# A hybrid decoder layer on one core: column order, chain engines, inverse blocks and PSUM tiles of the RWKV stage rewritten

## The chip, the cores and the metric

The kernel runs on one core of one Trainium2 chip. The metric is the device time of one launch in microseconds (us). A kernel's time is the median of its runs; beside it there is one execution taken with the hardware profiler, whose own time can differ a little from the median.

## The reference

One layer of a decoder for a prompt of 1024 rows and for 8 single decode rows, all in float32. The rows are normalised and go through one projection `w_in` (1024 to 3480 columns). Its columns feed three groups of heads:

- NSA: 8 query heads with compressed, selected and sliding-window attention, mixed by gates.
- RWKV-7: 4 heads with a state of 64 x 64 each.
- memory: 4 heads that attend to 256 memory rows.

Each group's output is multiplied by the SiLU of its gate columns; one output projection follows, and the residual is added. The part that matters here is the RWKV group, which the reference computes row by row:

```python
u = u_cur + (prev - u_cur) * mu            # token shift
r, k, v, wl, al = split(u)
decay = exp(-exp(w)); a = sigmoid(a0 + al @ a2)
def step(s, inp):
    r_t, k_t, v_t, w_t, kk_t, b_t = inp
    sa = einsum('bhvk,bhk->bhv', s, -kk_t)
    s = s * w_t + sa[..., None] * b_t + v_t[..., None] * k_t
    return s, einsum('bhvk,bhk->bhv', s, r_t)
```

Queries and keys of the other groups get a root-mean-square norm per head of 64, a gain, and rotary positions (rope).

## The kernel before

Phase 1 does the projection and the RWKV group; phase 2 the attention of the prompt, with most of the decode rows as side work; phase 3 the rest of the decode rows.

**Projection.** The 1024 prompt rows are taken in two halves H of 512. A column block of 128 is loaded by `wblock` (L227 on): one DMA of 512 KB, then the float32 weights are split into a high part on ScalarE (whi, L236) and a low part (wlo, L238), six eighths of it on GpSimd and two on VectorE. `project` (L241 on) runs eight steps; in each the three products hi*hi, hi*lo and lo*hi of one eighth of the 1024 inputs are added into PSUM. The p_pr tiles come from a pool of three one-bank buffers; a column needs two of them for H = 0 (512 prompt and 8 decode rows) and one for H = 1. After the eighth step the column is evicted: `do_u` for the seven RWKV columns (ScalarE copies, VectorE adds the shifted row, and the copy to ulast, L283, is last), `to_tok` for the others (ScalarE copies; later, in the next column's third step, four TensorE transposes to token order and then `kv_rows` or `norm_rope` and a DMA to DRAM), or `do_z` for gate columns.

**Norm and rope.** `norm_rope` (L307 on) squares on ScalarE, sums and takes the reciprocal root on VectorE, multiplies by it on VectorE (L323), by the gain on GpSimd (L324), and makes four products with sine and cosine on GpSimd (L334 to L337), which VectorE combines (L338, L339).

**RWKV in chunks.** The prompt is taken in four chunks Q of 256 rows. `rwkv_prep` (L572 on) makes the scaled rows and the masked product matrix AM; some of its elementwise steps run on GpSimd. `rwkv_state` (L682 on) inverts eight triangular matrices of 64 x 64. They are held as blocks of 32; five rounds double the inverted size (p_iy, then p_it with the new inverse T and its transpose Tt in one tile), and two more products join the blocks of 32 (tile iO, L745). The inverse is applied in p_x (L769 to L773), and four steps of 64 rows carry the state Z (p_z, L807 to L811). U, the RWKV input, holds two chunks: its first half is projected before chunk 0, its second half while chunk 1's state runs.

**The order of the work.** From chunk 0 until the fill is used up, TensorE's instructions are chained in the order in which the program emits them (class `InOrder`, whose helper line is L83 in the profile). The other engines are ordered by the framework's planner. `drive` (L489 on) runs a chunk's generator: each `yield n` says how long the chain behind it needs, and 1.3 n units of other columns (the fill, 0.7 units per step) are emitted there. Of the 21 column blocks outside RWKV, 16 are fill; what is left after chunk 3 is emitted in one go. `rwkv_out` (normalisation of the chunk's output) is emitted inside the next chunk's prep.

**The end of phase 1.** The last five columns run with background work of 41 steps (keys, compression, and memory keys, `ahead`, L478): after each group of eight column steps, BG = 4 background steps are emitted. Then phase 2 starts with the scores of its first tile and the compressed scores p_sc (L1151).

Of the kernel before, what the change touches and what calls it, by code (L numbers as in the profile page):

```python
# [31 lines left out]
BG = 4  # L32
# [70 lines left out]
class Step:  # L103
# [203 lines left out]
    def norm_rope(self, x, gain, nt, nh, rope, parts=128, psum=True):  # L307
# [16 lines left out]
        nc.gpsimd.tensor_tensor(y, y, bc(self.gains[:parts, gain:gain + 1, :], [parts, n, 64]), op=OP.mult)  # L324
# [4 lines left out]
        y4 = y.rearrange("p (t h) (s e) -> p t h s e", h=nh, s=2)  # L329
        o4 = o.rearrange("p (t h) (s e) -> p t h s e", h=nh, s=2)  # L330
        s4 = sq.rearrange("p (t h) (s e) -> p t h s e", h=nh, s=2)
        sh = [parts, nt, nh, 32]
        cos, sin = bc(cs[..., 0:32], sh), bc(cs[..., 32:64], sh)
        nc.gpsimd.tensor_tensor(s4[:, :, :, 0], y4[:, :, :, 1], sin, op=OP.mult)  # L334
        nc.gpsimd.tensor_tensor(s4[:, :, :, 1], y4[:, :, :, 0], sin, op=OP.mult)
        nc.gpsimd.tensor_tensor(o4[:, :, :, 0], y4[:, :, :, 0], cos, op=OP.mult)
        nc.gpsimd.tensor_tensor(o4[:, :, :, 1], y4[:, :, :, 1], cos, op=OP.mult)  # L337
        nc.vector.tensor_tensor(o4[:, :, :, 0], o4[:, :, :, 0], s4[:, :, :, 0], op=OP.subtract)  # L338
        nc.vector.tensor_tensor(o4[:, :, :, 1], o4[:, :, :, 1], s4[:, :, :, 1], op=OP.add)  # L339
# [52 lines left out]
    def phase1(self):  # L392
# [8 lines left out]
        with ExitStack() as ctx:  # L401
# [104 lines left out]
    def columns(self, tiles):  # L506
        rest = None
        for c0, do, j in tiles:
            m = 24 if j is None else 128
            hi, lo = self.wblock(c0, m)  # L510
            for H in range(2):
                out = []
                for k, n in enumerate(self.project(H, hi, lo, m, out)):
                    yield n
                    if k == REST and rest:
                        rest()
                rest = do(H, out, j)
        if rest:
            rest()
# [19 lines left out]
    def rwkv_open(self):  # L539
# [26 lines left out]
        for j, n in enumerate(("rwkv_ln_w", "rwkv_ln_b")):  # L566
            src = I[n]
            nc.scalar.dma_start(self.lnw[:, j, :], bass.AP(tensor=src.tensor, offset=src.offset, ap=[[0, 128], [1, 256]]))
        self.Z = c.tile([128, 2, 128], F32, name="Z0", tag="Z", bufs=2)
        nc.gpsimd.memset(self.Z[:], 0.0)  # L570

    def rwkv_prep(self, q):  # L572
# [28 lines left out]
        G.tensor_copy(swp(vs[:])[:, :, ::-1, :], swp(v))  # L601
# [4 lines left out]
        G.tensor_tensor(lw[:], L[:], lw[:], op=OP.subtract)  # L606
# [7 lines left out]
        yield 2.0  # L614
# [14 lines left out]
        yield 1.0  # L629
# [19 lines left out]
        ar = self.ar = self.rr.tile([128, 2, 2, 2, 2, 64], F32, name="ar")  # L649
        bk = self.bk = self.rr.tile([128, 2, 4, 2, 64], F32, name="bk")  # L650
        kt = lambda x: x.rearrange("p c (t e) -> p (c t) e", e=128)
        av = ar[:].rearrange("p c t k s e -> p (c t) k (s e)")
        sp = lambda x: x.rearrange("p c (n s e) -> p (c n) s e", s=2, e=64)
        bv = bk[:].rearrange("p c (n s) k e -> p (c n) s k e", s=2)
        G.tensor_tensor(av[:, :, 1, :], kt(r), kt(eL[:]), op=OP.mult)
        for p in range(2):
            G.tensor_tensor(bv[:, :, p, 1 - p, :], sp(kp[:])[:, :, p, :], sp(eN[:])[:, :, p, :], op=OP.mult)
# [12 lines left out]
        for t in range(2):  # L670
            for hp in range(2):
# [7 lines left out]
                for p in range(2):  # L679
                    V.tensor_tensor(amv[:, t, hp, p], ps[:, p], bc(self.maskA[:, None, :], [128, 2, 128]), op=OP.mult)  # L680

    def rwkv_state(self, Q):  # L682
# [7 lines left out]
        for (g, o, p, b), e in zip(blocks, (V, G, V, G)):  # L690
            x = AM[o, 2 * p:2 * p + 2, :, b * 32:b * 32 + 32]
            e.tensor_tensor(x, x, bc(self.eye[o, None, None, :], [32, 2, 4, 32]), op=OP.add)
# [11 lines left out]
        for i in range(5):  # L704
# [24 lines left out]
            new = self.ri.tile([128, 2, 8, 32], F32, name="iT", bufs=2)  # L729
            ps = self.pw.tile([128, 2, 8, 32], F32, name="p_it", tag="w")  # L730
            for t, h, j in th if i else ():
                for g, o, p, b in blocks:
                    PE.matmul(ps[o, 0, j, :], Tt[o, j, :], Y[o, j, :], start=True, stop=True)
            for t, h, j in th:
                for g, o, p, b in blocks:
                    PE.matmul(ps[o, 1, j, :], Y[o, j, :], Tt[o, j, :] if i else I[o, o], start=True, stop=True)
            if i:
                A.activation(new[:], ps[:], AF.Copy)
            else:
                A.activation(new[:, 1], ps[:, 1], AF.Copy)  # L740
            T, Tt = new[:, 0] if i else Y, new[:, 1]
            yield 1.0

        lo, up = [blocks[0][1], blocks[2][1]], [blocks[1][1], blocks[3][1]]
        off = self.ri.tile([128, 8, 32], F32, name="iO")  # L745
        for p in range(2):
            G.tensor_copy(off[up[p]], Tt[up[p]])
# [5 lines left out]
        A.activation(Y[up[0]], ps[up[0]], AF.Copy)  # L753
# [3 lines left out]
        for t, h, j in th:  # L757
            for p in range(2):
                PE.matmul(ps[lo[p], j, :], Y[up[p], j, :], Tt[up[p], j, :], start=True, stop=True)
        A.activation(off[lo[0]], ps[lo[0]], AF.Copy)  # L760
        V.tensor_copy(off[lo[1]], ps[lo[1]])
# [1329 lines left out]
```

## Time and profile before

| | us |
|---|---|
| median of 3 runs | 1236.52 |
| lowest and highest | 1236.21, 1238.66 |
| the profiled execution | 1246.17 |
| its span in the profile | 1244.4 |

| engine | busy us | share of the span |
|---|---|---|
| TensorE (PE) | 1103.6 | 89% |
| VectorE (DVE) | 708.5 | 57% |
| ScalarE (ACT) | 459.2 | 37% |
| GpSimd (POOL) | 327.0 | 26% |

PEld is TensorE's loading of weights, which overlaps its matmuls. A row of a timeline has the start and the length in us, the engine, the line, the operation and its tiles, and in brackets how long the engine stood idle before and what ended that. A row of a list of waits has the total, the number and the longest. A row of a group has the busy time, the mean in ns, and the idle time before. Matmuls overlap in their pipeline, so the starts of successive rows say more than their lengths.

### The profile page before, as it was taken

Reading aid. Unit: us, or ns where it says so; the run is one execution under the profiler, and the core shown is the slowest. Engines: PE = TensorE matmul, PEld = TensorE weight load, DVE = VectorE, ACT = ScalarE, POOL = GpSimd, SP = SyncE. Lnnn points to the kernel's source line nnn. Section 1 sums busy time; section 2 is a strip of 40 time slices with the busy share of each in tenths; the row PEclk is TensorE's granted clock in tenths of the full one; section 3 lists DMA queues with packets and bytes.
Section 4 is the critical chain, followed back from the end, with each engine's and each line's share of the span. In section 5 each row is a group of like instructions: output and inputs, shape, how many; then the busy total and the mean of one; then the engine's idle time right before and its main releaser. Section 6 shows DMA issues by size and latency. Waiting matters only on the chain. (4 is left out here: it accounts for less than half of the span.)

```text
span 1244.4 us, 27882 instructions
## 1 busy us (share of the span) xinstructions
PE 1103.6 (89%) x11547; PEld 874.2 (70%) x11547; DVE 708.5 (57%) x1939; ACT 459.2 (37%) x1003; POOL 327.0 (26%) x370
## 2 busy tenths in 40 slices
PE   5998897887788998999998999899999799799998
PEld 4877676655577777687886666677677577677776
DVE  7546167234263575454343788757568887465572
ACT  6341222211222132122332554555565466424420
POOL 3434115113162141233111223212221732111000
PEclk9998998888799998999999899999999999899999
DMA  7312102110112034024616301333310023735321
GB/s 229 89 47 67 32 21 83 44 36 26 51 43 63 19 112 94 14 69 110 169 53 197 100 2 39 115 106 89 84 39 7 25 90 101 243 118 197 120 82 62
DMA packets 124037, 102.28 MB, mean 82 GB/s; under 512 B 33455, under 2 KB 109646, under 8 KB 121734
## 3 DMA queue, kind: packets, MB, share of 16 engines
q1 hardware_dynamic: 119846, 82.50, 22.7%
q0 software_dynamic: 2304, 16.78, 3.9%
q8 instruction: 91, 1.49, 0.5%
q10 hardware_dynamic: 1760, 1.21, 0.3%
q14 instruction: 36, 0.29, 0.1%
HBM read 81.88 MB, written 22.78 MB: 84 GB/s over the span
## 5 line engine op out<-in xcount | busy, mean ns | idle before, releaser
L83 PE MATMUL p_pr<-h,whi 128*128 128x256 f32 (+3 forms) x880 | 221.9, 359 | 20.6 <-DVE ulast L283 19.2
L83 PEld LDWEIGHTS p_pr<-h,whi 128*128 128x128 f32 (+1 forms) x880 | 141.0, 196 | 40.8 <-issue 23.2
L83 PE MATMUL p_pr<-h,wlo 128*128 128x512 f32 (+5 forms) x440 | 130.7, 345 | 1.4 <-POOL wlo L238 1.4
L238 POOL TENSOR_TENSOR wlo<-wraw,whi 128x768 fp32r<-128x768 f32 (+1 forms) x35 | 68.4, 1955 | 176.9 <-ACT whi L236 160.5
L1254 POOL TENSOR_TENSOR p<-p,fac 128x640 f32<-128x640 f32 (+4 forms) x64 | 61.8, 986 | 187.2 <-DVE fac L1248 86.2
L248 PE MATMUL p_pr<-h,whi 128*128 128x256 f32 (+2 forms) x464 | 93.7, 308 | 3.3 <-DVE ulast L283 1.9
L1274 PE MATMUL p_o<-pt,vs 128*64 128x128 f32 x1056 | 90.0, 287 | 3.9 <-ACT pt L1196 1.5
L83 PEld LDWEIGHTS p_pr<-h,wlo 128*128 128x128 f32 (+1 forms) x440 | 77.7, 196 | 12.4 <-POOL wlo L238 2.2
L1192 PE MATMUL p_pT<-ident,p 128*128 128x128 f32 x528 | 85.1, 291 | 1.2 <-DVE pt L1198 0.7
L1219 PE MATMUL p_s<-kh,qs 128*128 128x512 f32 (+3 forms) x192 | 78.2, 408 | 8.4 <-ACT p L1236 8.1
L236 ACT ACTIVATE whi<-wraw 128x1024 fp32r<-128x1024 f32 (+1 forms) x35 | 36.4, 1039 | 124.4 <-PE p_pr L83 73.9
L248 PEld LDWEIGHTS p_pr<-h,whi 128*128 128x128 f32 x464 | 70.6, 190 | 8.1 <-issue 4.2
L1274 PEld LDWEIGHTS p_o<-pt,vs 128*64 128x64 f32 x1056 | 57.7, 137 | 26.1 <-issue 15.0
L1192 PEld LDWEIGHTS p_pT<-ident,p 128*128 128x128 f32 x528 | 59.6, 146 | 18.2 <-issue 15.2
L324 POOL TENSOR_TENSOR nr_y<-nr_y,gains 128x512 f32<-128x512 f32 (+4 forms) x26 | 27.0, 1037 | 171.0 <-DVE nr_y L323 150.2
L1236 ACT ACTIVATE p<-p_s,nm 128x640 f32<-128x640 f32 (+3 forms) x64 | 55.8, 872 | 38.4 <-DVE nm L1235 36.5
L1235 DVE TENSOR_REDUCE nm<-p_s 128x1 f32<-128x640 f32 (+3 forms) x64 | 58.6, 918 | 16.0 <-PE p_s L1222 15.6
L1220 PE MATMUL p_s<-kl,qs 128*128 128x512 f32 (+3 forms) x192 | 66.4, 350 | 0.0
L1196 ACT ACTIVATE pt<-p_pT 128x512 f32<-128x512 f32 (+1 forms) x72 | 42.6, 591 | 59.2 <-PE p_pT L1192 58.8
L248 PE MATMUL p_pr<-h,wlo 128*128 128x256 f32 (+2 forms) x232 | 61.8, 306 | 0.7 <-POOL wlo L238 0.7
L238 DVE TENSOR_TENSOR wlo<-wraw,whi 128x256 fp32r<-128x256 f32 (+1 forms) x35 | 19.9, 569 | 73.4 <-ACT whi L236 73.3
L1198 DVE COPY pt<-p_pT 128x512 f32<-128x512 f32 (+1 forms) x72 | 47.7, 663 | 20.6 <-PE p_pT L1192 20.2
(533 smaller groups left out, 2450.3 us busy)
## 6 DMA issues: line engine op xcount, KB each, us to landing
wraw<-in_w_in_dram SPq DMA_DIRECT2D x34, 512.0 KB
x<-in_x_prompt_dram SPq DMA_DIRECT2D x8, 512.0 KB
z_d<-zt SPq DMA_DIRECT2D x16, 256.0 KB
cat<-z_d SPq DMA_DIRECT2D x8, 512.0 KB
wor<-in_w_out_dram SPq DMA_DIRECT2D x16, 256.0 KB
xres<-in_x_prompt_dram SPq DMA_DIRECT2D x16, 256.0 KB
out_dram<-xres SPq DMA_DIRECT2D x16, 256.0 KB
out_dram<-in_cache_win_dram SPq DMA_DIRECT2D x8, 511.0 KB
```

Source lines behind the costliest of these rows:

```text
L83: self.last = getattr(self.engine, op)(*a, **k)
L238: e.tensor_tensor(lo[:, z, :n], raw[:, z, :n], hi[:, z, :n].bitcast(F32), op=OP.subtract)
L248: self.last_mm = self.pe.matmul(ps[:m, :b - a], w[:, k, :m], h[k][:, a:b], start=(k == 0 and i == 0), stop=(k == 7 and i == 2))
L1192: nc.tensor.transpose(ps[:, j, :], src(j), self.ident[:])
L1196: nc.scalar.activation(pt[:, :n], ps[:, :n], AF.Copy)
L1198: nc.vector.tensor_copy(pt[:, :n], ps[:, :n])
L1219: PE.matmul(ps, q, self.kh[u][:, 2 * b + g, o:o + w], start=True, stop=False)
L1220: PE.matmul(ps, q, self.kl[u][:, 2 * b + g, o:o + w], start=False, stop=not masks)
L1235: V.tensor_reduce(nm[:, h, b:b + 1], ps[:, c0:n1], axis=AX.X, op=OP.max, negate=True)
L1236: A.activation(Ps[h, b][:, :n1 - c0], ps[:, c0:n1], AF.Exp, bias=nm[:, h, b:b + 1], accum_out=sm[:, h, b:b + 1])
L1254: nc.gpsimd.tensor_tensor(x, x, bc(f[:, h, b:b + 1], x.shape), op=OP.mult)
L1274: PE.matmul(po[h * 64:h * 64 + 64], self.vs[k // 4][:, k % 4, b, g], pt[:, 2 * m + h], start=(n == 0 and m == 0), stop=False)
```

## The change

1. `columns`: the eviction follows the eighth step at once instead of at the next request, and a flag `open` tells whether a column is between its first step and its eviction. Before the second U half is started, the fill is run until no column is open.
2. `norm_rope`: the gain and the four rope products go from GpSimd to VectorE. The copy of kv columns without norm goes from VectorE to ScalarE.
3. `rwkv_prep`: GpSimd's steps go to VectorE (rk, the difference in lw, the products into ar and bk, which also move ahead of the first matmuls) and ScalarE (the square, the copy vs). Waiting units grow from 2.0 to 2.5 and from 1.0 to 1.2, and after each of the four p_am groups stands a new `yield 0.5`.
4. `rwkv_state`: both additions of the diagonal that ran on GpSimd go to VectorE. In the five rounds, T and its transpose get a PSUM tile each, with a new `yield 0.6` between them and 0.7 instead of 1.0 after them. The last round's transpose is copied straight into Ti, a tile of 64 x 64 blocks, and the joining product's result into its corner; p_x then is one product of 64 x 64 for each matrix instead of a 32-row and a 64-row product.
5. p_z: both halves are multiplied in one accumulation group before either is read.
6. BG goes from 4 to 6.

```diff
-BG = 4
+BG = 6
...
-        nc.gpsimd.tensor_tensor(y, y, bc(self.gains[:parts, gain:gain + 1, :], [parts, n, 64]), op=OP.mult)
+        nc.vector.tensor_tensor(y, y, bc(self.gains[:parts, gain:gain + 1, :], [parts, n, 64]), op=OP.mult)
...
-        nc.gpsimd.tensor_tensor(s4[:, :, :, 0], y4[:, :, :, 1], sin, op=OP.mult)
-        nc.gpsimd.tensor_tensor(s4[:, :, :, 1], y4[:, :, :, 0], sin, op=OP.mult)
-        nc.gpsimd.tensor_tensor(o4[:, :, :, 0], y4[:, :, :, 0], cos, op=OP.mult)
-        nc.gpsimd.tensor_tensor(o4[:, :, :, 1], y4[:, :, :, 1], cos, op=OP.mult)
+        V = nc.vector
+        for s in range(2):
+            V.tensor_tensor(s4[:, :, :, s], y4[:, :, :, 1 - s], sin, op=OP.mult)
+            V.tensor_tensor(o4[:, :, :, s], y4[:, :, :, s], cos, op=OP.mult)
...
-            nc.vector.tensor_copy(o[:], ps[:])
+            nc.scalar.copy(o[:], ps[:])
...
                 if Q == 1:
+                    while self.open:
+                        next(fill)
                     second = self.u_half(1)
...
                 out = []
+                self.open = True
                 for k, n in enumerate(self.project(H, hi, lo, m, out)):
-                    yield n
+                    if k < 7:
+                        yield n
                     if k == REST and rest:
                         rest()
                 rest = do(H, out, j)
+                self.open = False
+                yield STEP
...
-            G.tensor_scalar(rk[:, c, :], r[:, c, :], self.v("rwkv_r_k", c), None, op0=OP.mult)
-        G.tensor_tensor(sq[:], kk[:], kk[:], op=OP.mult)
+            V.tensor_scalar(rk[:, c, :], r[:, c, :], self.v("rwkv_r_k", c), None, op0=OP.mult)
+        A.activation(sq[:], kk[:], AF.Square)
...
-        G.tensor_copy(swp(vs[:])[:, :, ::-1, :], swp(v))
+        A.copy(swp(vs[:])[:, :, ::-1, :], swp(v))
...
-        G.tensor_tensor(lw[:], L[:], lw[:], op=OP.subtract)
+        V.tensor_tensor(lw[:], L[:], lw[:], op=OP.subtract)
...
-        yield 2.0
...
+        V.tensor_tensor(av[:, :, 1, :], kt(r), kt(eL[:]), op=OP.mult)
+        for p in range(2):
+            V.tensor_tensor(bv[:, :, p, 1 - p, :], sp(kp[:])[:, :, p, :], sp(eN[:])[:, :, p, :], op=OP.mult)
+        yield 2.5
...
                     V.tensor_tensor(amv[:, t, hp, p], ps[:, p], bc(self.maskA[:, None, :], [128, 2, 128]), op=OP.mult)
+                yield 0.5
...
-        for (g, o, p, b), e in zip(blocks, (V, G, V, G)):
+        for g, o, p, b in blocks:
...
+            if i:
+                ps = self.pw.tile([128, 8, 32], F32, name="p_it", tag="w")
+                for t, h, j in th:
+                    for g, o, p, b in blocks:
+                        PE.matmul(ps[o, j, :], Tt[o, j, :], Y[o, j, :], start=True, stop=True)
+                A.activation(new[0][:], ps[:], AF.Copy)
+                yield 0.6
+            ps = self.pw.tile([128, 8, 32], F32, name="p_it", tag="w")
...
+            if i < 4:
+                A.activation(new[1][:], ps[:], AF.Copy)
             else:
-                A.activation(new[:, 1], ps[:, 1], AF.Copy)
+                for g, o, p, b in blocks:
+                    (V.tensor_copy if g % 2 else A.copy)(self.Ti[o, :, b * 32:b * 32 + 32], ps[o])
+            T, Tt = new[0] if i else Y, new[1]
+            yield 0.7
...
-                for p in range(2):
-                    PE.matmul(px[lo[p], h, :], Tt[lo[p], j, :], R[lo[p], h, :], start=True, stop=True)
                 for p in range(2):
                     o = slice(p * 64, p * 64 + 64)
-                    PE.matmul(px[up[p], h, :], off[o, j, :], R[o, h, :], start=True, stop=True)
+                    PE.matmul(px[o, h, :], Ti[o, t * 4 + h, :], pre[t][o, h, :], start=True, stop=True)
...
                     PE.matmul(pz[:, c, :], bkT[t][:, c, p, :], UV[:, n, 2 * c:2 * c + 2, :].rearrange("p a b -> p (a b)"),
-                              start=True, stop=False)
-                    PE.matmul(pz[:, c, :], PT[t][:, c, p, :], Z[:, c, :], start=False, stop=True)
+                              start=(c == 0), stop=False, skip_group_check=True)
+                for c in range(2):
+                    PE.matmul(pz[:, c, :], PT[t][:, c, p, :], Z[:, c, :], start=False, stop=(c == 1), skip_group_check=True)
+                for c in range(2):
                     V.scalar_tensor_tensor(Zn[:, c, :], pz[:, c, :], self.gC[:, c, n:n + 1], self.blockm,
```

More of the change, by code (lines that the diff above doesn't have):

```diff
@@ L568, in rwkv_open @@
             nc.scalar.dma_start(self.lnw[:, j, :], bass.AP(tensor=src.tensor, offset=src.offset, ap=[[0, 128], [1, 256]]))
+        self.Ti = c.tile([128, 8, 64], F32, name="Ti")
+        nc.gpsimd.memset(self.Ti[:], 0.0)
         self.Z = c.tile([128, 2, 128], F32, name="Z0", tag="Z", bufs=2)
@@ L613, in rwkv_prep @@
         V.tensor_copy(gC[:], eL[:].rearrange("p c (n t) -> p c n t", t=64)[:, :, :, 63])
-        yield 2.0
+        ar = self.ar = self.rr.tile([128, 2, 2, 2, 2, 64], F32, name="ar")
+        bk = self.bk = self.rr.tile([128, 2, 4, 2, 64], F32, name="bk")
+        kt = lambda x: x.rearrange("p c (t e) -> p (c t) e", e=128)
+        av = ar[:].rearrange("p c t k s e -> p (c t) k (s e)")
+        sp = lambda x: x.rearrange("p c (n s e) -> p (c n) s e", s=2, e=64)
+        bv = bk[:].rearrange("p c (n s) k e -> p (c n) s k e", s=2)
+        V.tensor_tensor(av[:, :, 1, :], kt(r), kt(eL[:]), op=OP.mult)
+        for p in range(2):
+            V.tensor_tensor(bv[:, :, p, 1 - p, :], sp(kp[:])[:, :, p, :], sp(eN[:])[:, :, p, :], op=OP.mult)
+        yield 2.5
         UV = self.UV = self.rr.tile([128, 4, 4, 64], F32, name="UV")
@@ L628, in rwkv_prep @@
         V.tensor_copy(s8[:], ps8[:8, :256])
-        yield 1.0
+        yield 1.2
         pst = self.pw.tile([128, 512], F32, name="p_s8t", tag="w")
@@ L728, in rwkv_state @@
             yield 0.7
[L729 to L733, printed above, removed]
+            new = [self.ri.tile([128, 8, 32], F32, name="iT", tag=f"iT{j}", bufs=2) for j in range(2)]
+            if i:
[6 more added lines that the diff above has]
+            ps = self.pw.tile([128, 8, 32], F32, name="p_it", tag="w")
             for t, h, j in th:
                 for g, o, p, b in blocks:
-                    PE.matmul(ps[o, 1, j, :], Y[o, j, :], Tt[o, j, :] if i else I[o, o], start=True, stop=True)
-            if i:
-                A.activation(new[:], ps[:], AF.Copy)
-            else:
-                A.activation(new[:, 1], ps[:, 1], AF.Copy)
-            T, Tt = new[:, 0] if i else Y, new[:, 1]
-            yield 1.0
+                    PE.matmul(ps[o, j, :], Y[o, j, :], Tt[o, j, :] if i else I[o, o], start=True, stop=True)
+            if i < 4:
+                A.activation(new[1][:], ps[:], AF.Copy)
+            else:
+                for g, o, p, b in blocks:
+                    (V.tensor_copy if g % 2 else A.copy)(self.Ti[o, :, b * 32:b * 32 + 32], ps[o])
+            T, Tt = new[0] if i else Y, new[1]
+            yield 0.7
         lo, up = [blocks[0][1], blocks[2][1]], [blocks[1][1], blocks[3][1]]
-        off = self.ri.tile([128, 8, 32], F32, name="iO")
-        for p in range(2):
-            G.tensor_copy(off[up[p]], Tt[up[p]])
+        Ti = self.Ti
         ps = self.pw.tile([128, 8, 32], F32, name="p_iy", tag="w")
@@ L752, in rwkv_state @@
         Y = self.ri.tile([128, 8, 32], F32, name="iY", bufs=2)
-        A.activation(Y[up[0]], ps[up[0]], AF.Copy)
+        A.copy(Y[up[0]], ps[up[0]])
         V.tensor_copy(Y[up[1]], ps[up[1]])
@@ L758, in rwkv_state @@
             for p in range(2):
-                PE.matmul(ps[lo[p], j, :], Y[up[p], j, :], Tt[up[p], j, :], start=True, stop=True)
-        A.activation(off[lo[0]], ps[lo[0]], AF.Copy)
-        V.tensor_copy(off[lo[1]], ps[lo[1]])
+                PE.matmul(ps[lo[p], j, :], Y[up[p], j, :], Ti[up[p], j, 32:64], start=True, stop=True)
+        A.copy(Ti[lo[0], :, 32:64], ps[lo[0]])
+        V.tensor_copy(Ti[lo[1], :, 32:64], ps[lo[1]])
         yield 0.8
@@ L764, in rwkv_state @@
         for t in range(2):
-            R = pre[t]
             px = self.pw.tile([128, 4, 128], F32, name="p_x", tag="w")
             for h in range(4):
-                j = t * 4 + h
-                for p in range(2):
-                    PE.matmul(px[lo[p], h, :], Tt[lo[p], j, :], R[lo[p], h, :], start=True, stop=True)
                 for p in range(2):
                     o = slice(p * 64, p * 64 + 64)
-                    PE.matmul(px[up[p], h, :], off[o, j, :], R[o, h, :], start=True, stop=True)
+                    PE.matmul(px[o, h, :], Ti[o, t * 4 + h, :], pre[t][o, h, :], start=True, stop=True)
             W[t] = self.rs.tile([128, 4, 64], F32, name="W", tag=f"W{t}")
```

16 lines of the change are left out of this document (4 added, 12 removed).

## The prediction

> **What bounds the kernel now.** I read the page first: the span, TensorE's busy time and the clock that it was granted.
>
> ```profile
> span 1244.4 us, 27882 instructions
> PE 1103.6 (89%) x11547; PEld 874.2 (70%) x11547; DVE 708.5 (57%) x1939; ACT 459.2 (37%) x1003; POOL 327.0 (26%) x370
> PEclk9998998888799998999999899999999999899999
> ```
>
> TensorE works in 89% of the span, so time can only come out of its 140.8 us of idle time, out of stretches at a low clock (the eights and the seven in the first half), or out of matmuls that go away. Then I cut the span by stages of the program: prep and state of RWKV chunk 0 and prep 1 (75 to 226 us); state 1 with the second U half (226 to 340); chunks 2 and 3 (340 to 535); the late columns with the background work (582 to 673); the start of attention (673 to 697).
>
> ```profile
> 75.00:226.00 151.00, 131.10 (x1887) 108.36 (x1886) 82.73 (x247) 35.70 (x75) 50.97 (x52) 0.93 0.18 50
> 226.00:340.00 114.00, 87.97 (x1245) 65.95 (x1244) 35.08 (x102) 20.82 (x37) 22.00 (x18) 0.85 0.13 36
> 340.00:535.00 195.00, 173.53 (x3010) 139.78 (x3009) 103.73 (x325) 46.82 (x97) 59.14 (x61) 0.96 0.20 55
> ...
> 582.00:673.00 91.00, 87.39 (x562) 75.41 (x561) 32.44 (x76) 30.66 (x63) 15.08 (x21) 1.00 0.43 122
> 673.00:697.00 24.00, 15.58 (x60) 9.71 (x60) 18.41 (x52) 9.71 (x19) 3.91 (x4) 0.77 0.71 199
> ```
>
> The columns are the stage, its length, the busy time of PE, PEld, DVE, ACT and POOL, the granted clock, and DMA. The three RWKV stages have 19.9, 26.0 and 21.5 us of idle TensorE. What the low clock costs I take as busy time times what is missing of the clock: 9.2, 13.2 and 6.9 us, and 3.6 us in the last row. Next, who TensorE waits for between 95 and 545 us (total, times, longest):
>
> ```profile
> PE p_pr L83 <- DVE ulast L283: 18.9, 6, 3.7
> PE p_it L83 <- issue: 10.2, 8, 2.5
> PE p_z L83 <- DVE Zn L811: 7.5, 16, 0.5
> PE p_s8t L83 <- DVE s L628: 7.5, 2, 6.5
> PE p_ul L83 <- DVE ul L526: 3.8, 1, 3.8
> PE p_vt L83 <- POOL vs L601: 3.7, 3, 1.6
> PE p_rs L83 <- DVE rq_t L124: 2.9, 1, 2.9
> ...
> PE p_rs L83 <- DVE rsb L639: 2.7, 1, 2.7
> PE p_am L83 <- DVE rq_r L125: 2.5, 1, 2.5
> PE p_am L83 <- DVE AM L680: 2.1, 1, 2.1
> ```
>
> Nearly all of these waits lie in code that the change touches. The order of TensorE is fixed by hand here, so each wait holds all that is queued behind it.
>
> **The U columns.** With a column of H = 0 open, two of the three p_pr buffers are held, and all seven U columns of the second half share the third: six waits for the eviction's last step, ulast. TensorE's timeline there:
>
> ```profile
> 304.03 0.62 PE L83 MATMUL p_pr<-h,whi 128*128 128x512 f32 x2
> 304.50 0.39 PE L83 MATMUL p_pr<-h,wlo 128*128 128x512 f32 x1
> 304.73 0.63 PE L83 MATMUL p_pr<-h,whi 128*128 128x512 f32 x2
> ...
> 310.64 1.19 PE L83 MATMUL p_pr<-h,whi 128*128 128x512 f32 x2 [3.65 <-DVE ulast L283]
> ...
> 312.05 1.06 PE L83 MATMUL p_pr<-h,whi 128*128 128x512 f32 x2
> ```
>
> A step takes 0.70 us (304.03 to 304.73) and 1.41 us right after the wait (310.64 to 312.05): the wait also brings the low clock. Draining the open column first gives U three buffers with one tile each, so a column starts while the one before is evicted. The drained steps (at most seven) only move. Gain: 18.9 us of waits, and of the stage's 13.2 us of clock about 11; the rest belongs to the p_ul wait (3.8 us), which stays, since the last U column is still followed by its transpose. Sum 30. Next late would be the weights: a column then takes 5.6 us (8 x 0.70), and the conversion to lo on GpSimd takes 2.0 us of that (row 198.21 below), so they are hidden. Lower bound: 18.9 us, if the clock stays low for other reasons.
>
> **GpSimd's part of the chains.** Why p_s8t waits 6.5 us is seen on VectorE and GpSimd just before it:
>
> ```profile
> 197.60 0.92 DVE L338 TENSOR_TENSOR nr_o<-nr_o,nr_sq 128x256 f32<-128x256 f32 x1 [3.31 <-POOL nr_o L336]
> 198.45 2.02 DVE L339 TENSOR_TENSOR nr_o<-nr_o,nr_sq 128x256 f32<-128x256 f32 x1
> 200.39 0.40 DVE L628 COPY s<-p_s 8x256 f32<-8x256 f32 x1
> 198.21 1.98 POOL L238 TENSOR_TENSOR wlo<-wraw,whi 128x768 fp32r<-128x768 f32 x1
> ```
>
> VectorE stands 3.31 us for GpSimd's rope products and then runs one step for 2.02 us beside GpSimd's wlo. The copy s that the RWKV chain needs queues behind both. After the change the rope needs no hand-over. Prices on VectorE for 512 and 256 elements, with GpSimd's mean for the gain step (1.04 us) beside them:
>
> ```profile
> L323 DVE TENSOR_TENSOR nr_y<-p_tk,rq_r 128x512 f32<-128x512 f32 x13 | 9.0, 690 | 0.7 <-DVE rq_r L125 0.2
> L833 DVE TENSOR_TENSOR y_c<-y_c,gn_s 128x256 f32<-128x256 f32 x8 | 3.4, 420 | 0.1
> L324 POOL TENSOR_TENSOR nr_y<-nr_y,gains 128x512 f32<-128x512 f32 (+4 forms) x26 | 27.0, 1037 | 171.0 <-DVE nr_y L323 150.2 <-DVE rq_r L125 9.9 <-DVE rq_t L123 5.7
> ```
>
> One norm with rope adds 0.69 + 4 x 0.42 = 2.4 us to VectorE. There are twelve such half columns (28 us) and four without rope (2.8 us). Per RWKV chunk come two rk, one lw, one ar, two bk and two diagonal additions: 2 x 0.69 + 6 x 0.42 = 3.9 us, 16 us in all. Eight kv copies at about 0.69 us leave for ScalarE, which is busy 103 of 460 us and hides them. VectorE thus goes from 221.5 busy us (sum of the three stages) to about 263, in some 395 us: two thirds, with room on average but not everywhere.
>
> The prep waits sum to 7.5 + 3.7 + 2.9 + 2.7 + 2.5 + 2.1 = 21.4 us. All stand behind GpSimd or a VectorE that it held. The new yields put about 5 more fill steps into each prep (2.7 units x 1.3 / 0.7). I take 13 us of the 21.4 as gone, and 8 of the 16.1 us of clock in the first and third stage. Bounds 3 and 37. Against this I set 8 us for places where a rope batch on VectorE now stands ahead of a chain step; no row shows it, it lies between 0 and the 41 us added.
>
> A rule that speaks against the move: the Trainium skill, SBUF — State Buffer, section Who interferes with whom, says that a VectorE instruction with two SBUF inputs contends with a GpSimd instruction that reads SBUF. By that rule wlo, which stays on GpSimd, will hold more VectorE steps than now. The 2.02 us step beside wlo, 0.42 elsewhere, agrees with it; what such holds would cost here is priced with the first rival.
>
> **p_z.** Before, the second half's first matmul waits for Zn to be read from the bank of the first half: 16 waits, 7.5 us. Now both halves are multiplied before either is read; Zn is next needed only after the p_yy products and the next chunk step's bkT products. All 7.5 us go; I count 8 with the restart. Least 5.
>
> **p_x.** Before, per chunk 16 groups alternate between 32- and 64-row tiles; now 16 matmuls of 64 x 64, in 32 instructions where there were 64.
>
> ```profile
> 153.84 0.41 PE L83 MATMUL p_x<-R,iT 32*32 32x128 f32 x4
> ...
> 159.26 0.66 PE L83 MATMUL p_tk<-ident,ct 128*128 128x128 f32 x4
> ...
> 161.21 0.45 PE L83 MATMUL p_g<-AM,W 64*64 64x64 f32 x8
> ```
>
> The old stretch is 159.26 - 153.84 = 5.4 us. The nearest row, eight 64 x 64 instructions of half the width in 0.45 us (0.056 each), gives 32 x 0.056 = 1.8 us, or 3.6 at double. Four chunks save 7 to 14 us; I take 12, since the halves use separate tiles.
>
> **The inverse's iterations.** The matmuls are as many, but T and its transpose come in two groups of 64 with fill between, where 128 ran in one go. The waits named issue (10.2 us at p_it) fall inside those long groups; I take 5 off, bounds -4 and 10. Assembling Ti in place costs nothing on the path: the four small copies (0.42 us each, two per engine) are not needed by the next product, which reads T.
>
> **More changes of tile shape.** Four more interludes in a prep and four in a state, 32 in all. Entering one:
>
> ```profile
> 125.95 0.40 PE L83 MATMUL p_pr<-h,wlo 128*128 128x256 f32 x2
> 126.28 0.72 PE L83 MATMUL p_it<-iY,iT 32*32 32x32 f32 x62
> ```
>
> wlo to the next start is 0.33 us instead of 0.23 (304.50 to 304.73); the same again on leaving makes 0.2 us, so 32 x 0.2 = 6 us lost. The fill itself is the same work: +3.6 units x 1.3 / 0.7 = 6.7 steps per chunk, 27 steps or 19 us taken from the fill that is left after chunk 3.
>
> The Trainium skill, TensorEngine Tiling (Array Packing), section Key Properties, says that a change of tiling mode drains TensorE. If a drain cost as much as the 0.39 us of one wide matmul (row 304.50), 64 changes would cost 25 us; the row here gives 0.10 a change.
>
> **Background at 6 steps.** Its 41 steps were spread over ten groups of 4, so the memory keys ended with the last column:
>
> ```profile
> 680.34 0.42 DVE L323 TENSOR_TENSOR nr_y<-p_mo,rq_r 128x256 f32<-128x256 f32 x1 [2.83 <-DMA out_dram<-nr_y]
> 680.91 0.77 PE L1151 MATMUL p_sc<-qs,ckh 128*128 128x512 f32 x1 [5.12 <-DVE nr_y L323]
> ```
>
> Attention's first products wait 5.1 us for that tail, then run at a low clock (3.6 us). At 6 steps the tail ends in the seventh group, three groups early. I count 7 gained: 8.7 less about 1.5 for the last column's own eviction. Bounds -5 (denser background waits for its DMAs: 582 to 673 has only 3.6 us idle today) and 9.
>
> **Sum.** -30 - 13 - 8 + 8 - 8 - 12 - 5 + 6 - 7 = -69 us. The profiled execution took 1246.17 us (its span and 1.8 us around it), 0.8% over the median of 1236.52. Scaled to it: 1236.5 x (1246.2 - 69) / 1246.2 = 1168 us.
>
> **The rivals.** First, VectorE becomes the bound in the preps. For: it is busy 82.7 of 151 us in the first stage, the rope comes in one block, and wlo still runs beside it: a step held for 2.02 instead of 0.42 us is 1.6 us late. Against: much of today's busy time is such holding. If each of the 16 norm batches, by its length or by wlo, keeps TensorE 2 us more, 32 us come back: 1236.5 - 37 = 1200 us. Second, each change of shape costs as much as a wide matmul, 0.39 us: 25 instead of 6 us lost, about 1187 us. For it speaks only the count of changes, against it the 0.10 us of the row. Third, the change does not do what it says for U: the columns start on time but wait for weights, since a block of 512 KB must land and be converted every 5.6 us instead of every 11; the 30 us stay, about 1198 us. Fourth, slower: VectorE executes in order, and if whole batches stand right ahead of a step of the inverse's chain, each costs the batch (0.69 x 3 + 6 x 0.42 + 2 us of small rsqrt steps = 6.6 us) less about 1.3 us of fill, 5.3, and then some 1.3 us of low clock. That is 6.6 us each; from 11 of the 16 batches on, it outweighs 69 us, and with all 16 (106 us) the time is about 1272 us. Against it: today the same batches, with their holds, stand in no wait for iY.
>
> **Chances.** Forecast 0.62; VectorE bound 0.16; U not freed 0.09; drains 0.07; slower 0.06. The forecast's own range is 1148 to 1190. The range for 8 in 10 reaches to 1204, over the first three rivals, and down to 1138, about 98 us, where nearly all waits and clock go. Under 0.2%, 2.5 us, is no change for this kernel. Faster 0.92, same 0.02, slower 0.06.
>
> **What would show it.** Right: no ulast wait in state 1 and U columns every 5.6 us; the 226 to 340 stage shorter by 30 us at a clock near 1; no p_z wait; p_x under 3.6 us a chunk; no 5 us wait at the first p_sc; GpSimd's rope lines gone. Wrong: TensorE waiting for VectorE at p_s8t, p_rs, p_am or p_it in sum over 25 us, waits for wlo at p_pr in U, or more issue time at p_it.

## The result, and the profile after

The changed kernel takes 1186.92 us (median of 4 runs, 1183.26 to 1189.12). The kernel before took 1237.59 us beside it (median of 4, 1236.21 to 1243.97). The ratio is 0.9578, with a 95% interval of 0.9534 to 0.9622: 50.7 us less, where 1168 us had been forecast in a range of 1138 to 1204. The profiled execution took 1185.08 us, 61.1 us less than the profiled execution before. The medians differ by 10 us less than that, because the profiled execution before lay 8.6 us above its own median and the one after 1.8 us below.

The page of the changed kernel, as far as it answers to the rows of before:

```profile
span 1183.3 us, 27621 instructions
PE 1083.9 (92%) x11419; PEld 862.9 (73%) x11419; DVE 728.7 (62%) x2073; ACT 472.4 (40%) x1039; POOL 216.6 (18%) x221
PEclk9999999998899999899999999999999899999999
```

TensorE's idle time fell from 140.8 us to 1183.3 - 1083.9 = 99.4. The same stretches of time as before, cut from the changed kernel (stretch, length, busy PE, PEld, DVE, ACT and POOL, granted clock, DMA share, GB/s); since everything ends earlier now, the second holds more work and the third some of the left-over columns:

```profile
75.00:226.00 151.00, 142.08 (x2020) 119.70 (x2018) 99.14 (x324) 44.59 (x97) 18.32 (x12) 0.97 0.20 57
226.00:340.00 114.00, 97.95 (x1260) 75.08 (x1260) 50.73 (x151) 31.32 (x58) 20.76 (x15) 0.93 0.17 48
340.00:535.00 195.00, 183.38 (x3041) 150.73 (x3040) 110.21 (x380) 50.38 (x113) 25.96 (x25) 0.96 0.26 70
```

Idle TensorE is 8.9, 16.1 and 11.6 us (19.9, 26.0 and 21.5 before). The clock's price, counted as in the prediction, is 4.3 + 6.9 + 7.3 = 18.5 us, where it was 29.3. Who TensorE waits for, from 75 to 640 us (total, times, longest):

```profile
PE p_pr L83 <- POOL wlo L238: 8.2, 6, 2.4
PE p_iy L83 <- DVE AM L702: 5.2, 7, 2.2
PE p_pr L83 <- ACT whi L236: 4.1, 5, 1.0
PE p_ul L83 <- DVE ul L533: 3.8, 1, 3.8
PE p_rs L83 <- DVE rsb L657: 3.5, 2, 3.3
PE p_vt L83 <- ACT vs L610: 3.1, 2, 2.4
PE p_s8t L83 <- DVE s L646: 2.6, 2, 1.7
...
PE p_iy L83 <- issue: 2.1, 2, 1.4
PE p_it L83 <- issue: 1.8, 4, 0.7
```

The ulast, p_z and p_am waits are gone, issue fell from 12.9 to 3.9 us, and the prep waits from 21.4 to 3.5 + 3.1 + 2.6 = 9.2. On top stands something new: TensorE waits for weights, wlo and whi, 12.3 us in all. TensorE's timeline shows where:

```profile
291.05 0.40 PE L83 MATMUL p_pr<-h,wlo 128*128 128x512 f32 x1
292.40 0.73 PE L83 MATMUL p_pr<-h,whi 128*128 128x512 f32 x2 [0.96 <-ACT whi L236]
294.53 0.50 PE L83 MATMUL p_pr<-h,wlo 128*128 128x512 f32 x1 [1.39 <-POOL wlo L238]
294.87 0.62 PE L83 MATMUL p_pr<-h,whi 128*128 128x512 f32 x2
...
295.57 0.63 PE L83 MATMUL p_pr<-h,whi 128*128 128x512 f32 x2
...
300.89 0.74 PE L83 MATMUL p_pr<-h,whi 128*128 128x512 f32 x2 [0.96 <-ACT whi L236]
303.01 0.80 PE L83 MATMUL p_pr<-h,wlo 128*128 128x512 f32 x1 [1.39 <-POOL wlo L238]
303.61 1.05 PE L83 MATMUL p_pr<-h,whi 128*128 128x512 f32 x2
...
304.89 1.05 PE L83 MATMUL p_pr<-h,whi 128*128 128x512 f32 x2
...
313.68 1.20 PE L83 MATMUL p_pr<-h,whi 128*128 128x512 f32 x2
```

Up to 309.49 these are the last two U columns. They no longer wait for an eviction, but they start 8.5 us apart (292.40 to 300.89), not 5.6; the column before them took 12.1 us, from 280.30. The timelines of ScalarE and GpSimd say why the weights are late:

```profile
291.29 1.06 ACT L236 ACTIVATE whi<-wraw 128x1024 fp32r<-128x1024 f32 x1 [4.59 <-PE p_pr L83]
299.78 1.06 ACT L236 ACTIVATE whi<-wraw 128x1024 fp32r<-128x1024 f32 x1 [6.85 <-PE p_pr L83]
...
292.43 2.05 POOL L238 TENSOR_TENSOR wlo<-wraw,whi 128x768 fp32r<-128x768 f32 x1 [5.73 <-ACT whi L236]
```

The conversion isn't slow, it starts late, and TensorE releases it: 291.29 is when the matmuls of the column before have ended (the last starts at 291.05). Converted weights have two buffers (the pool of whi and wlo). The drain stops when the column's half H = 0 is evicted; the block's half H = 1 is still to come, so the block keeps one of the two buffers through all U columns. The seven columns share the other, and a column waits for its predecessor's end, then 1.06 us for whi and some 2 for wlo. The kept half H = 1 follows right behind the U columns: the last row above of TensorE (313.68) is its first step. The longest single wait, 2.4 us, has a second cause: there wlo starts at 281.58, 1.3 us after its whi has ended, because GpSimd is still at three steps on y_c that began at 279.27.

The program's marks in the profiled executions (start, us):

| | before | after |
|---|---|---|
| p_ul, behind the last U column | 333.9 | 313.6 |
| last p_yy of chunk 3 | 534.7 | 511.4 |
| close of RWKV (p_s, L851 and L862) | 581.9 | 532.7 |
| first attention product | 672.8 | 627.5 |
| first p_out | 1055.5 | 999.8 |
| span | 1244.4 | 1183.3 |

At the close of RWKV 49.2 us are won; all but the background part of the 69 had been expected there, 62. The late columns then take 94.8 instead of 90.9 us.

### The profile page after: what moved, and what is told of

Same layout as the page of the kernel before. It is cut to its first block, busy times and chain, and to the rows that moved or that the text cites. A ratio compares the mean times of both kernels' runs of the same rounds, so it can differ in the third digit from the quotient of the medians.

```text
span 1183.3 us, 27621 instructions
## 1 busy us (share of the span) xinstructions
PE 1083.9 (92%) x11419; PEld 862.9 (73%) x11419; DVE 728.7 (62%) x2073; ACT 472.4 (40%) x1039; POOL 216.6 (18%) x221
## 4 chain that ended last, share of the span: by engine, by line
PE 49%; DVE 16%; DMA 5%; ACT 2%; issue 2%; POOL 0%; DVEq 0%; SPq 0%; ACTq 0%; POOLq 0%
PE p_pr L83 7%; PE p_pT L1203 5%; PE p_o L1285 5%; PE p_out L1962 4%; PE p_pr L248 4%; PE p_s L1230 2%; DMA wor<-in_w_out_dram 2%; PE p_s L1231 2%; DMA xg<-in_cache_nsa_dram,idx 2%; PE p_hid L929 1%; DVE nm L1246 1%; PE p_it L83 1%; DVE p L1263 1%; PE p_q L1142 1%; PE p_o L1289 1%
## 5 line engine op out<-in xcount | busy, mean ns | idle before, releaser
L83 PE MATMUL p_pr<-h,whi 128*128 128x256 f32 (+3 forms) x880 | 221.1, 357 | 4.4 <-ACT whi L236 4.1
L83 PEld LDWEIGHTS p_pr<-h,whi 128*128 128x128 f32 (+1 forms) x880 | 136.7, 192 | 25.4 <-ACT whi L236 6.0
L83 PE MATMUL p_pr<-h,wlo 128*128 128x512 f32 (+5 forms) x440 | 129.7, 343 | 8.2 <-POOL wlo L238 8.2
L1285 PE MATMUL p_o<-pt,vs 128*64 128x128 f32 x1056 | 92.5, 286 | 3.8 <-ACT pt L1207 1.5
L83 PEld LDWEIGHTS p_pr<-h,wlo 128*128 128x128 f32 (+1 forms) x440 | 76.3, 192 | 20.4 <-POOL wlo L238 10.8
L236 ACT ACTIVATE whi<-wraw 128x1024 fp32r<-128x1024 f32 (+1 forms) x35 | 36.3, 1038 | 85.9 <-PE p_pr L83 55.5
L1962 PE MATMUL p_out<-wol,chi 128*128 128x512 f32 x128 | 51.6, 403 | 0.2 <-DVE wol L1952 0.2
```

Of the source, the lines that this page charges most:

```text
L83: self.last = getattr(self.engine, op)(*a, **k)
L1285: PE.matmul(po[h * 64:h * 64 + 64], self.vs[k // 4][:, k % 4, b, g], pt[:, 2 * m + h], start=(n == 0 and m == 0), stop=False)
L1962: nc.tensor.matmul(po[:rows], c[:, k, :rows], w[:], start=(k == 0 and j == 0), stop=(k == 7 and j == 2))
```

## The experiments

Each ratio is to the kernel before on the same chip (median 1238.1 to 1240.9 us), with its 95% interval; 0.001 is 1.24 us.

**The drain taken out** (the rest of the change stays):

```diff
-                    while self.open:
-                        next(fill)
                     second = self.u_half(1)
```

> The changed kernel without the draining before the second U half (the eviction still follows the eighth step at once). If the open column's PSUM buffers were what held U, the six ulast waits of some 3 us come back and the waits for whi and wlo at p_pr go back under 2 us in sum: ratio to the kernel before 0.970 to 0.978 (15 to 25 us slower than the change). If U is now bound by its weights whatever the drain does, the ratio stays at 0.958 to 0.962.

1195.13 us, 0.9652 (0.9608 to 0.9695). All the other parts together bring 3.5%, 43 us. The drain brings 0.9652 - 0.9578 = 0.0074, 9 us (2 to 17 by the two intervals). In this profile the U columns wait for ulast again:

```profile
PE p_pr L83 <- DVE ulast L283: 22.5, 6, 6.4
```

No wait for weights is left there. So the drain exchanges a 22.5 us wait for one of 12.3 us.

**The drain to the end of the block.** If the kept buffer is the cause, the drain has to go on until H = 1 is done too:

```diff
-                self.open = False
+                if H == 1:
+                    self.open = False
                 yield STEP
```

> The changed kernel, but the fill runs until both halves of the open column block are done, not only the half that is open. Theory: the U columns wait for whi (4.1 us) and wlo (8.2 us) because the drained block still has its second half to do and keeps one of the two weight slots, so that a U column's weights are converted only when the column before has ended. Then these waits fall under 2 us, U columns follow at 5.6 us, and the 225 to 314 us stage is 12 to 17 us shorter: ratio 0.944 to 0.949. Rival: ScalarE and GpSimd themselves are too slow for a column every 5.6 us, or their queues hold the conversion behind other work: waits and ratio as in the change, 0.958.

1166.18 us, 0.9403 (0.9373 to 0.9433): 21 us less than the changed kernel. No U column waits any more. ScalarE converts ahead: the second conversion here starts 7.5 us after the first, while TensorE is still in the column before, and ScalarE doesn't stand idle ahead of it:

```profile
279.07 1.06 ACT L236 ACTIVATE whi<-wraw 128x1024 fp32r<-128x1024 f32 x1 [1.49 <-PE p_pr L83]
286.60 1.04 ACT L236 ACTIVATE whi<-wraw 128x1024 fp32r<-128x1024 f32 x1
```

and TensorE goes in steps of 0.70 us without a gap from 276.25 to the end of the last U column. What follows it (row 299.81, with 256 columns and not 512) is the half H = 0 of a new block, no kept half:

```profile
294.45 0.63 PE L83 MATMUL p_pr<-h,whi 128*128 128x512 f32 x2
294.92 0.40 PE L83 MATMUL p_pr<-h,wlo 128*128 128x512 f32 x1
295.16 0.63 PE L83 MATMUL p_pr<-h,whi 128*128 128x512 f32 x2
...
299.81 1.22 PE L83 MATMUL p_pr<-h,whi 128*128 128x256 f32 x4
```

p_ul comes at 299.8 instead of 313.6, chunk 3 ends at 498.5 instead of 511.4. That settles the weights, and this version beats both kernels. That blocks can't land and be converted every 5.6 us, as the third rival had it, is refuted for these columns: with both buffers free none waits. Against the run without a drain it is 0.9652 - 0.9403 = 0.0249, 31 us (24 to 37). In the two profiles the waits at L83 fall from 46.2 to 27.9 us (75 to 545 us) and the clock's price in the three stretches from 23.2 to 11.0.

**The U part alone**, on top of the kernel before, with the drain to the end of the block:

> The kernel before with one part alone: open columns are drained ahead of the U columns, until both halves of the block are done. If the U columns' waits are a cost of their own, this part is worth what it was worth in the changed kernel (1195.1 without a drain, 1166.2 with the drain to the end of the block, so 29 us): a ratio of 0.974 to 0.979 to the kernel before, no ulast wait and no wait for whi or wlo in the U columns. If instead the older, sparser order gives the time back later (fill that was drained early is missing in the next chunk's gaps), the waits go and the ratio stays above 0.985.

1225.69 us, 0.9886 (0.9845 to 0.9927): 14 us (9 to 19), against the 31 us of the drain inside the change, although this part also holds the eviction right after the eighth step, which the 31 us don't. The waits for ulast went, but others came in their place:

```profile
PE p_s8t L83 <- DVE s L635: 9.7, 2, 6.5
PE p_z L83 <- DVE Zn L818: 8.7, 16, 1.6
PE p_it L83 <- issue: 7.0, 8, 1.8
PE p_it L83 <- DVE iY L718: 5.5, 3, 3.6
...
PE p_iy L83 <- DVE AM L699: 3.7, 2, 3.2
```

Waits for iY (5.5 here, 1.5 at another line) had no row before, and AM at p_iy had 0.3 us. From 75 to 545 us TensorE's waits sum to 54.2 us, where they were 67.4; 18.9 went and about 6 net came back. That slow U columns had covered these chain steps, and fast ones don't, fits, but wasn't tested by itself. These two profiles can't decide it either: the executions that they show differ by 1246.17 - 1217.92 = 28 us, twice what the medians do. Why the part is worth less alone stays open.

**Rope and gain back on GpSimd** (six instructions of a norm with rope; the first of them shown):

```diff
-        nc.vector.tensor_tensor(y, y, bc(self.gains[:parts, gain:gain + 1, :], [parts, n, 64]), op=OP.mult)
+        nc.gpsimd.tensor_tensor(y, y, bc(self.gains[:parts, gain:gain + 1, :], [parts, n, 64]), op=OP.mult)
```

> The changed kernel with the gain and the four rope products on GpSimd again. Theory of the prediction: VectorE stands for GpSimd again and RWKV chain steps queue behind; p_s8t, p_rs, p_am and p_iy waits grow by 8 to 15 us, some low clock on top: ratio 0.966 to 0.976. Rival: VectorE was already the tight engine in the preps and is relieved by 31 us of work, so the waits for the diagonal (5.2 us at p_iy) go and the time falls: ratio 0.950 to 0.956.

1214.02 us, 0.9778 (0.9743 to 0.9814): rope on VectorE is worth 0.0200, 25 us (18 to 32), more than expected. The waits that come back:

```profile
PE p_rs L83 <- DVE rsb L657: 7.9, 3, 4.2
PE p_am L83 <- DVE AM L689: 5.7, 1, 5.7
PE p_it L83 <- DVE iY L721: 4.8, 1, 4.8
...
PE p_am L83 <- DVE rq_r L125: 1.9, 1, 1.9
```

From 75 to 545 us the waits rise from 36.3 to 50.3 us, and the clock falls with them:

```profile
226.00:340.00 114.00, 93.64 (x1323) 70.76 (x1324) 44.22 (x118) 29.29 (x53) 23.54 (x19) 0.88 0.15 41
340.00:535.00 195.00, 177.24 (x2969) 148.26 (x2968) 102.59 (x341) 46.06 (x102) 45.72 (x49) 0.92 0.22 61
```

With 0.97 in the first stage the clock costs 138.3 x 0.03 + 93.6 x 0.12 + 177.2 x 0.08 = 29.6 us, 11 more than in the changed kernel. Waits and clock make 14 + 11 = 25 us. The groups of VectorE show what the hand-over also costs on VectorE; first here, then in the changed kernel (busy us, mean ns):

```profile
L338 DVE TENSOR_TENSOR nr_o<-nr_o,nr_sq 128x256 f32<-128x256 f32 (+4 forms) x19 | 15.1, 794 | 27.1 <-POOL nr_o L337 27.0
L339 DVE TENSOR_TENSOR nr_o<-nr_o,nr_sq 128x256 f32<-128x256 f32 (+4 forms) x19 | 10.6, 557 | 5.3 <-POOL nr_o L337 5.3
```

```profile
L338 DVE TENSOR_TENSOR nr_o<-nr_o,nr_sq 128x256 f32<-128x256 f32 (+4 forms) x19 | 7.0, 367 | 0.0
L339 DVE TENSOR_TENSOR nr_o<-nr_o,nr_sq 128x256 f32<-128x256 f32 (+4 forms) x19 | 6.7, 352 | 0.0
```

The two last steps of the rope take 794 and 557 ns when GpSimd makes the products, 367 and 352 when it doesn't. These means mix two kinds of steps. With the products on GpSimd, all twelve steps of 128x256 at L338 run beside a GpSimd step and take 0.93 to 0.95 us, one of them 2.07; at L339 the nine that run beside none take 0.41 to 0.43, the three others 0.94, 2.03 and 2.05. In the changed kernel 23 of these 24 steps take 0.41 to 0.42 us. Being side by side doesn't always cost: three of the 23 (92.46, 92.80 and 211.28) run while the profile shows a wlo on GpSimd.

**The prep's steps back on GpSimd** (rk, sq, vs, lw, ar, bk; their new place in the code stays):

```diff
-        A.copy(swp(vs[:])[:, :, ::-1, :], swp(v))
+        G.tensor_copy(swp(vs[:])[:, :, ::-1, :], swp(v))
```

> The changed kernel with the prep's elementwise steps (rk, the square, vs, the difference in lw, the products into ar and bk, at their new place) on GpSimd again; norm and rope stay on VectorE. If the GpSimd steps themselves held the chain, p_vt, p_s8t and p_rs waits grow by 5 to 12 us: ratio 0.962 to 0.969. If only the rope blocked VectorE, nothing changes (0.956 to 0.960), or VectorE's relief gains up to 4 us.

1187.59 us, 0.9587 (0.9565 to 0.9609): no difference, to within some 6 us. With the rope on VectorE, it doesn't matter more than that which engine makes these steps.

**Two of the four diagonal additions back on GpSimd**, to see if they cause the new wait of p_iy for AM:

```diff
-        for g, o, p, b in blocks:
+        for (g, o, p, b), e in zip(blocks, (V, G, V, G)):
...
-            V.tensor_tensor(x, x, bc(
+            e.tensor_tensor(x, x, bc(
```

> The changed kernel with two of the four diagonal additions on GpSimd again. The new waits of p_iy for the diagonal (5.2 us) should fall to about 1 us if the four additions in a row on VectorE make them: ratio 0.953 to 0.957. If they come from VectorE's queue ahead of the additions, they stay: 0.957 to 0.959.

1181.36 us, 0.9527 (0.9497 to 0.9557), with single runs from 1174.7 to 1189.2. The time came out about where it had been expected if these additions made the wait, but the wait didn't go: 5.8 us in its profile. The interval overlaps that of the changed kernel, and below, on the better drain, the same edit brings nothing. So the additions aren't shown to cost anything.

**The old inverse and p_x on top of the change:**

```diff
-            new = [self.ri.tile([128, 8, 32], F32, name="iT", tag=f"iT{j}", bufs=2) for j in range(2)]
+            new = self.ri.tile([128, 2, 8, 32], F32, name="iT", bufs=2)
...
-                    PE.matmul(px[o, h, :], Ti[o, t * 4 + h, :], pre[t][o, h, :], start=True, stop=True)
+                for p in range(2):
+                    PE.matmul(px[lo[p], h, :], Tt[lo[p], j, :], R[lo[p], h, :], start=True, stop=True)
```

> The changed kernel with the old rounds (T and its transpose in one tile, one group of 128 products, yields 0.7 and 1.0), the old joining and the old p_x of 32- and 64-row tiles; everything else as in the change. The p_x stretch should take 5.4 instead of 1.9 us per chunk (14 us) and the issue waits at p_it and p_iy grow from 3.9 to about 13 us, less 3 us for the fewer changes of shape: 18 to 24 us slower, ratio 0.973 to 0.978. If the changes of shape cost a full drain, the fewer of them give back more: under 12 us slower, ratio under 0.968.

1191.84 us, 0.9614 (0.9578 to 0.965): 4 us, and not clear of the noise (some 7 us). But no U column waits for weights in this profile: with the old yields the drain happens to end behind a half H = 1 (the U columns are followed by 128x256 matmuls, a half H = 0, at 301.53). Two effects of opposite sign lie on top of each other here, so the run says little. The clean test has the drain to the end of the block in both:

> Block drain as in the run at 1166.2 us, but with the old rounds of the inverse, its old joining and the old p_x. In the run with the old inverse on top of the change, the U columns happened to be free of weight waits, which hid the price. Here the U columns are free either way. The trace's terms (p_x 5.4 instead of 1.9 us in four chunks, 14 us; issue 9 us; less about 1 us for the new waits at p_it) give 18 to 24 us: 1184 to 1190, ratio 0.955 to 0.960. If the finer inverse is worth only its p_x, 12 to 14 us: ratio 0.950 to 0.952. If it is worth no more than the 5 us that the run on top of the change showed: 0.944.

1194.97 us, 0.9635 (0.96 to 0.9669), against 0.9403 without the old inverse: 0.0232, 29 us (23 to 34). Issue is back:

```profile
PE p_it L83 <- issue: 13.8, 12, 2.7
PE p_iy L83 <- DVE AM L703: 5.4, 4, 3.0
...
PE p_iy L83 <- issue: 3.2, 5, 1.0
```

That is 17.0 us of issue, where the version with the new inverse has 4.8 (3.9 at p_it, 0.9 at p_iy). And p_x takes its old 5.4 us a chunk (154.18 to 159.59) instead of 1.9. 12 + 14 = 26 of the 29 us are accounted for. The clock's price is higher too, 17.4 instead of 11.0 us, which would make 32: the terms are good to some us only. The rounds and p_x weren't tested one without the other.

**The old p_z on top of the change:**

```diff
-                              start=(c == 0), stop=False, skip_group_check=True)
-                for c in range(2):
-                    PE.matmul(pz[:, c, :], PT[t][:, c, p, :], Z[:, c, :], start=False, stop=(c == 1), skip_group_check=True)
-                for c in range(2):
+                              start=True, stop=False)
+                    PE.matmul(pz[:, c, :], PT[t][:, c, p, :], Z[:, c, :], start=False, stop=True)
```

> The changed kernel with the old order at p_z (each half multiplied in its own group, the second half's products behind the first half's reading). The 16 waits of 0.45 us come back: 7 to 9 us slower, ratio 0.964 to 0.966. If that time was hidden elsewhere, no difference: 0.957 to 0.959.

1187.12 us, 0.9582 (0.9557 to 0.9607): no difference, though the 16 waits came back. The same edit on the other version:

> Block drain as in the run at 1166.2 us, with the old order of the p_z matmuls, so that the second half waits for Zn again (16 waits, 7.4 us). If these waits cost their length: 1173 to 1175, ratio 0.945 to 0.948. If most of it is given back later, as the run on top of the change suggested (no difference): 0.939 to 0.942.

1174.78 us, 0.9469 (0.9432 to 0.9505), against 0.9403: 8 us (2 to 14).

```profile
PE p_z L83 <- DVE Zn L821: 7.4, 16, 0.5
```

**Four background steps instead of six:**

```diff
-BG = 6
+BG = 4
```

> The changed kernel with 4 background steps per group as before. If the 6 steps are what moves the memory keys off the start of attention, the 5 us wait of the first p_sc and the low clock behind it come back and the columns' stage gets some 4 us shorter: 4 to 8 us slower, ratio 0.961 to 0.965. If the gain came from the earlier eviction of columns or from the profile's noise, no difference (0.957 to 0.959).

1186.34 us, 0.9544 (0.9501 to 0.9587): no difference; by the two intervals six steps bring between 3 us gained and 12 lost. The wait at the first p_sc is back, 5.0 us, but the late columns take 91.5 us (534.1 to 625.6) instead of 94.8, and TensorE's waits in them sum to 1.7 instead of 4.9 us. So the denser background pays back on the way some 3 us of what it gains at the end; where the rest goes isn't shown.

**The drain to the end of the block, with p_ul after state 1 and two diagonal additions on GpSimd:**

```diff
             self.do_u(H, out, j)
-        self.after_u(H)
...
                     for _ in second:
                         pass
+                    self.after_u(1)
```

> Block drain as in the run at 1166.2 us, with two more edits: the transpose p_ul is issued after state 1 instead of right behind the last U column, and two of the four diagonal additions are on GpSimd again. If the p_ul wait of 3.8 us costs its length and a clock of about 1.5 us, and the additions bring nothing: 1160 to 1162, ratio 0.935 to 0.937. If the additions are worth the 5 us that the medians showed: 0.931 to 0.933. If neither counts: 0.939 to 0.942.

1167.34 us, 0.9404 (0.9369 to 0.9439), the same as without both. The p_ul wait of 3.8 us stayed: the copy that p_ul needs was moved with it, so nothing lies between them in the new place either. This run speaks for the additions bringing nothing, and doesn't tell about p_ul; how much a p_ul without its wait would bring stays open.

## Why the prediction was right or wrong, step by step

The sign and the range were right; 1168 us missed by 19 us. The other parts had been set at 39 us and brought 43 (38 to 49). The error lies in the U columns: 30 us set, 9 measured. That 39 came so close to 43 is luck: the parts were set at 13 (GpSimd), 11 (p_x and the inverse, less the changes of shape), 8 (p_z) and 7 us (background). Tested one by one, they were worth 25 (rope and gain, in the changed kernel), 29 and 8 (on the better drain) and nothing. Two were set too low and one too high, and the single values add up to 62, not 43, so the parts mask each other.

**The step that failed** is "Next late would be the weights: a column then takes 5.6 us ..., and the conversion to lo on GpSimd takes 2.0 us of that ..., so they are hidden". It compared durations, 2.0 against 5.6 us, and didn't ask when the conversion may start. A conversion is hidden only if a second buffer is free, and the drained column's block held it. The sentences before it looked at the p_pr buffers and found what an open column holds there; its block holds weights too, and longer. The prediction's sign for it came true: waits for wlo at p_pr in U, 8.2 us, and 4.1 for whi. The third rival had this outcome ("waits for weights", about 1198 us), for another reason: the supply, which the run with the longer drain refutes. That run also shows that the size of 30 us was right: 31 us, at 1166 us in all, with 18.3 us of waits and 12.2 of clock in the profiles, where 18.9 and 11 had been set. But it's right only beside the other parts; alone the U part gives 14 us.

**Prep waits and clock.** The prep waits fell by 12.2 us, where 13 had been set. The new waits for VectorE (p_iy 5.2, p_it 1.2, p_at 0.5) make 7, where 8 had been set. VectorE's busy time in the three stretches is 260.1 us, where about 263 was forecast, but that is no confirmation: the stretches hold more work now. Over the whole span VectorE gained 20.2 us (708.5 to 728.7), where some 41 had been added. The clock's price fell by 10.8 us, where 11 + 8 had been set: by 6.3 in the stretch of the U columns, where behind some of the new weight waits a step takes 1.28 us (303.61 to 304.89) and not 0.70, and by 4.5 in the other two. That the whole GpSimd part is worth 13 us net was too little: the rope alone is worth 25, and the prep's steps nothing. The prediction set VectorE's price for the rope at 2.4 us a norm and counted no saving on the steps that stay there; the two at L338 and L339 fell from 13.9 + 11.6 us (before) to 7.0 + 6.7, 12 us of the 21 that are missing.

The Trainium skill, SBUF — State Buffer, section Who interferes with whom, had been weighed against the move: wlo on GpSimd would hold more VectorE steps. The traces bear out the interference, 0.93 to 2.07 us beside a GpSimd step and 0.41 to 0.43 beside none at L338 and L339, with the exceptions named there. But its sum went the other way: with the rope off GpSimd there is less of it.

**The first and the fourth rival** needed TensorE waiting for VectorE batches. New waits of 7 us came, where the rivals had set 32 and 106; at p_s8t, p_rs, p_am and p_it, whose sign of being wrong stood at 25 us, TensorE waits for VectorE for 7.3 us. **Drains at changes of shape** (second rival) are as small as the row had them. In the changed kernel's timeline

```profile
125.16 0.40 PE L83 MATMUL p_pr<-h,wlo 128*128 128x512 f32 x1
125.48 0.75 PE L83 MATMUL p_it<-iT,iY 32*32 32x32 f32 x64
126.17 0.73 PE L83 MATMUL p_pr<-h,whi 128*128 128x512 f32 x2
126.73 0.39 PE L83 MATMUL p_pr<-h,wlo 128*128 128x512 f32 x1
```

the way into p_it takes 0.32 us (125.16 to 125.48), where wide matmuls follow each other after 0.23, and the first pair behind it 0.56 (126.17 to 126.73) instead of 0.47: 0.2 us for both changes, as set.

**p_x and the inverse.**

```profile
151.75 1.96 PE L83 MATMUL p_x<-R,Ti 64*64 64x128 f32 x32
153.65 0.73 PE L83 MATMUL p_pr<-h,whi 128*128 128x512 f32 x2
```

1.90 us a chunk: the nearest row had given 1.8, and four chunks save 14 us where 12 had been taken. Issue fell by 9.0 us where 5 had been taken. Net of the changes of shape the prediction had 12 + 5 - 6 = 11 us here; the run with the longer drain and the old inverse gives 29.

**p_z** was right at 8 us (2 to 14) on the longer drain. On top of the change the same edit gave nothing (about 6 us either way); the two results overlap.

**Background** was wrong: 7 us set, 0 measured. The wait at p_sc went as said. The prediction's lower bound, that a denser background waits in the late columns, should have had the weight: the stretch grew by 3.9 us. But DMAs are the smaller part of it: beside the same kernel with four steps, TensorE waits there 1.2 us more for a DMA, 1.3 for kl and 0.9 for weights.

**The scale.** The prediction summed on a profiled execution of 1246.17 us and scaled by the ratio, which took only 0.5 us off. That execution was slow in a stretch that the change hardly touches: its attention and output take 571.6 us from the first product to the end, 564.0 in the profile of the U part alone, where that code is the same, and 555.8 in the changed kernel. So 15.8 of the 61.1 us between the two profiled executions lie there, where the prediction had 8.7 (the wait at p_sc and the clock behind it); the other 7.1 fit the 8.6 us by which the execution before lay above its median.

## What to carry to other kernels

Before a wait is called hidden, ask when the hidden work may start, not only how long it takes: list every buffer that an unfinished piece of work holds, weights as well as accumulators. Parts of a hand-made order don't add up (the U part: 14 us alone, 31 beside the rest; the old inverse: 4 us on the change, 29 on the longer drain), so test a part where nothing else masks it. And work that hands over between two engines can cost twice: the wait for the hand-over, and the longer steps of the engine that takes over while both run side by side.

## What the runs showed of the hardware

Waits on TensorE came with a loss of clock almost as large: with the rope on GpSimd, 14 us more of waits and 11 us more of lost clock; without the drain against the longer drain, 18 and 12. Small interruptions can be enough, and aren't always: gaps of 0.96 and 1.39 us stand in the first step of both U columns shown above, and the second goes on in steps of 1.28 us, the first in steps of 0.70. The Trainium skill, TensorE: Matmul & The Clock Gate, section Part 1, says that activity is watched in a free-running window, so that the same work can start at a low clock in one case and not in another; these two columns fit that, but no run here shows the window.

Executions of one kernel on one chip scatter by several us: 1183.3 to 1189.1 for the changed kernel, 1217.9 to 1231.0 for the U part alone, whose profiled execution was its fastest. The profiled executions lay up to 8.6 us above (before) and 7.8 us below (the U part alone) the medians of their kernels. A difference of two profiles of less than some 8 us is no result by itself.
